# Decoder trunk on one core: regrouping the last third of the down projections, and a new place for twelve conditioning columns

## The chip, the core and the metric

The kernel is one program on one NeuronCore of a Trainium2 chip. The metric is the device time of one execution, in microseconds, as the median of several runs. Besides that time there is one profiled execution, whose trace gives each instruction's start, length and engine: PE (TensorE matmuls), PEld (its weight loads), DVE (VectorE), ACT (ScalarE), POOL (GpSimd) and SP (SyncE, which here only issues DMAs).

## What is computed

The reference is a decoder trunk of two layers on a sequence of 512 tokens with 1024 channels. Each layer has three sub-layers, and each of them is normalised with a shift, a scale and a gate that come from a conditioning vector `c`:

```python
cond = jax.nn.silu(c)
for l in range(DEPTH):                                   # 2
    mod = cond @ ada_w[l] + ada_b[l]                     # 9 * 1024 values
    sh1, sc1, g1, sh2, sc2, g2, sh3, sc3, g3 = jnp.split(mod, N_MOD, axis=-1)
    h = modulate(x, norm_ffn1[l], sh1, sc1)
    x = x + 0.5 * (1.0 + g1)[:, None] * swiglu(h, ffn1_w1[l], ffn1_w3[l], ffn1_w2[l])
    h = modulate(x, norm_mix[l], sh2, sc2)
    y = token_mix(h, ...)          # gated delta rule and latent attention, two branches, gated, then w_out
    x = x + (1.0 + g2)[:, None] * y
    h = modulate(x, norm_ffn2[l], sh3, sc3)
    x = x + 0.5 * (1.0 + g3)[:, None] * swiglu(h, ffn2_w1[l], ffn2_w3[l], ffn2_w2[l])
```

`swiglu(h, w1, w3, w2)` is `(silu(h @ w1) * (h @ w3)) @ w2` with an inner width of 2816, that is 22 tiles of 128. `modulate` is an RMS norm over the channels, times a gain and `1 + scale`, plus a shift. Everything is in float32.

## The kernel before, in words

**Layout and precision.** Activations are held channel-major: a tile is 128 channels by 512 tokens. Every large product is done three times in the matmul's reduced fp32 type. Weights and activations are split into a high part (a cast on ACT) and a low part (a subtraction on DVE), and `mm3` adds high times high, high times low and low times high into one PSUM bank. A block of weights, called a slab, is 128 partitions by up to 1024 columns, that is up to eight blocks of 128x128, one for each `k` of a reduction. `slab` (L114) loads it with a DMA on SP's queue into a buffer `raw` (or `L`), and makes `whi` on ACT (L121) and `wlo` on DVE (L122), in two pieces of up to 512 columns each. There are two `raw`, three `whi`, three `wlo` and five `L` buffers.

**PSUM.** The eight banks are shared out by name: three `acc`, two `sm`, two `sc`, one `po` (`BUFS`).

**One FFN** (`ffn`). The 22 inner tiles are made in thirds of 8, 8 and 6. The tiles of a third are made by `pairs` (two inner tiles together, in seven products of half size, casts at L582 and L583 from slabs of 1024 columns, outputs to `x`, `y` and `z` in `acc`, `sm` and `sc`). The last step of a pair ends with a Silu of `x` on ACT (L633), a product on DVE (L638), and the split of the second inner tile (ACT L135, DVE L136). After each third, `down(i)` multiplies these inner tiles (`xs`, in buffers `O`) with the slabs of `w2`, one slab for each of the eight output tiles `m`, and adds the gated result to `x` (`residual`, L407, on DVE). This is done by `close`.

**`close`** (L410). For the first two thirds all eight `m` are done one after the other over all 512 tokens. For the last third four `m` are done so; the slabs of the other four are put into `spare` places in the buffers `A` (loaded through `L`), and these four are then done in two halves of 256 tokens, so that the norm of the first half can start while the second half is multiplied. The first half's banks are all `acc`, the second half's all `sc`. `finish` squares the new `x` on ACT (L320, L323) and adds the squares on DVE (L324). `NORM_AT` says after which `k` the norm's small matmuls are put in. `ahead` loads the next stage's first slabs. The same `close` with spare slabs in `O` does the output projection `w_out` at the end of the mixing.

**The conditioning columns.** A column of 128 values of `mod` is one `ada_block` (L264): a DMA of 512 KB into an `L` buffer and one DVE instruction (L269) that multiplies it with the conditioning vector `condb` (buffer `kph`) and sums. Its place in DVE's order is pinned by `order`. Per layer, 48 such columns (j from 2 to 7, eight each) wait in a queue before the first FFN; with layer 0's position tables that is 49 entries. `tick(n)` pops n of them at set places: two for each tile or pair of the upper projections, two or one for each output tile of the first two thirds, one for each of the last third's four. What is left is drained before the mixing.

**The order of the work.** The kernel is written with a scheduling layer. It takes instructions in the order in which they are written as priority, but an engine whose next instruction isn't ready by its estimate gets a later one that is, and a buffer goes to the instruction that asks for it when it comes free. The order so found is fixed in the program: on the chip each engine runs its list strictly in order, and each DMA queue too. `keep_in_program_order` (`order`, and `pin` for matmuls) puts an instruction behind the one that was written just before it for the same engine.

**The end of the mixing** (`mix`, L1267). After the attention, for each of eight tiles `m`: a slab of `w_branch_b`, a load of a stored gate, 24 matmuls, a product with the gate on DVE (L1416), an addition on POOL (L1417), and a split (L135, L136) into the buffers `A`. Then `x` comes back from memory and `close` does `w_out`. After the mixing `condb` is loaded again, since `kph` was lent to the attention.

Of the kernel before, what the change touches and what calls it, by code (L numbers as in the profile page):

```python
# [8 lines left out]
F32 = mybir.dt.float32  # L9
# [6 lines left out]
P = 128  # L16
SEQ = 512
D = 1024
# [16 lines left out]
HALVES = ((0, 256), (256, 512))  # L35
# [15 lines left out]

BEGIN_PE = (1, 2)

WQ, WK, WV, WZ, WLAT, WMISC, WGA, WGB = 0, 8, 16, 24, 32, 37, 38, 46
N_WIN = 54

# [17 lines left out]
class Trunk:  # L74
    def __init__(self, ctx, tc, aps):
        self.tc = tc
        self.nc = tc.nc
        self.ap = aps
        self.sb = ctx.enter_context(tc.tile_pool(name="sb", bufs=1))
        self.ps = ctx.enter_context(tc.tile_pool(name="ps", bufs=1, space=bass.MemoryType.PSUM))  # L80
        self.count = 0
        self.pin = False
        self.units, self.body, self.ahead = [], None, None
        self.queue = []
        self.waiting = []
        self.quarters = {}
# [24 lines left out]
        return self.ps.tile(list(shape), F32, tag=tag, name=f"{tag}_{self.count}", bufs=BUFS[tag])  # L111


    def slab(self, src, n, place=None, home="raw"):  # L114
        nc = self.nc
        raw = self.t(home, [P, 1024])
        hi, lo = place or (self.t("whi", [P, 1024], F32R), self.t("wlo", [P, 1024], F32R))
        nc.sync.dma_start(raw[:, :n], src)
        for a in range(0, n, 512):
            s = slice(a, min(a + 512, n))  # L120
            nc.scalar.copy(hi[:, s], raw[:, s])  # L121
            nc.vector.tensor_sub(lo[:, s], raw[:, s], hi[:, s].bitcast(F32))  # L122
        return hi, lo

    def mm3(self, out, w, x, start, stop):
# [137 lines left out]

    def ada_block(self, l, j, i, mod):  # L264

        raw = self.t("L", [P, D])
        self.nc.sync.dma_start(raw, self.ap["ada_w"][l, j, i])
        o = j * KT + i
        self.order(self.nc.vector.scalar_tensor_tensor(raw, raw, 1.0, self.condb, ALU.mult, ALU.mult,  # L269
                                                       accum_out=mod[:, o:o + 1]))  # L270
# [136 lines left out]
        self.nc.vector.scalar_tensor_tensor(self.x[:, m, a:b], ps[:, a:b], gate[:, m:m + 1], self.x[:, m, a:b],  # L407
                                            ALU.mult, ALU.add)

    def close(self, get, acts, gate, finish, spare=(), ahead=None, ticks=(1, 1)):  # L410

        late = KT - len(spare)
        for m in range(late):
            s = get(m)
            ps = self.p("acc")
            self.proj(ps, s, acts)
            self.residual(m, ps, gate, FULL[0])
            if finish is not None:
                finish(m, FULL[0])
            self.tick(ticks[m % 2])  # L420
# [1 line left out]
        if ahead is not None:  # L422
            ahead()
        norms = []
        for (a, b), tag in zip(HALVES if ws else (), ("acc", "sc")):
            for m, s in zip(range(late, KT), ws):
                ps = self.p(tag)
                n = len(acts)

                cut = NORM_AT.get(m - late, n) if norms else n  # L430
                self.proj(ps, s, acts, (a, b), range(cut))
                if cut < n:
                    next(norms[0], None)
                    self.proj(ps, s, acts, (a, b), range(cut, n))
                self.residual(m, ps, gate, (a, b))
                norm = finish(m, (a, b))
                if norm is not None:
                    norms.append(norm)
# [50 lines left out]
    def ffn(self, l, w, gate, finish, early, ahead=None):  # L489
# [199 lines left out]
        def down(i):  # L689
            k0, k1 = THIRDS[i]  # L690
            xs = [g[k] for k in range(k0, k1)]
            get = lambda m, place=None: self.slab(w2[l, m, :, k0:k1, :].rearrange("p k c -> p (k c)"), (k1 - k0) * P,
                                                  place, "L" if place else "raw")
            spare = []
            if i == 2:
                for _ in range(2):
                    sp = self.t("A", [P, 4, 1024], F32R)
                    spare += [(sp[:, 0], sp[:, 1]), (sp[:, 2], sp[:, 3])]
            self.close(get, xs, gate, finish if i == 2 else None, spare, ahead if i == 2 else None,
                       (1, 1) if i == 2 else (2, 1))  # L700

        begun = len(early) > 3
        plain = 6 if begun else 4
# [562 lines left out]

    def mix(self, l, vec, gate, finish, ws, ahead):  # L1267
        nc = self.nc
        xs = self.ap["spill"]
        for k in range(KT):  # L1270
            nc.sync.dma_start(xs[:, k, :], self.x[:, k, :])
# [132 lines left out]
        self.fill_all()  # L1404
        for cur in wait:
            next(cur, None)
        yh = self.t("A", [P, KT, SEQ], F32R)
        yl = self.t("A", [P, KT, SEQ], F32R)
        for m in range(KT):
            w = self.slab(self.ap["w_branch_b"][l, m].rearrange("p k c -> p (k c)"), 1024)  # L1410
            gate_b = self.t("c3", [P, SEQ])
# [4 lines left out]
            nc.vector.scalar_tensor_tensor(y, gate_b, 1.0, ps, ALU.add, ALU.mult)  # L1416
            nc.gpsimd.tensor_add(y, y, t1[0][:, m, :])  # L1417
            self.split(yh[:, m, :], yl[:, m, :], y)
        ys = [(yh[:, k, :], yl[:, k, :]) for k in range(KT)]
        self.x = self.t("M", [P, KT, SEQ])  # L1420
        for k in range(KT):
# [97 lines left out]
    def run(self, out):  # L1519
# [12 lines left out]
        for l in range(DEPTH):  # L1532
# [11 lines left out]

            for j in range(2, 8):
                self.queue += self.ada_chunk(l, j, vec, mod)
            if l == 0:
                self.queue.insert(10, self.rope_tables)
            g1 = {}
            self.ffn(l, "ffn1", _Lazy(lambda: self.set_gate(0, mod)), done(1, vec, mod),  # L1550
                     early if l == 0 else nxt["w"], then(self.mix_early, l))
            self.drain()
            self.mix(l, vec, self.set_gate(1, mod), done(2, vec, mod), nxt["w"], then(self.ffn_early, l, "ffn2"))
            self.condb = self.t("kph", [P, D])
            nc.sync.dma_start(self.condb, self.ap["spill_c"])
            self.queue += self.ada_chunk(l, 8, vec, mod)
            if l + 1 < DEPTH:
                nvec, nmod = self.layer_vectors(l + 1)
# [111 lines left out]
```

## Time and profile before

| | |
|---|---|
| median of 3 runs | 2739.33 us (2736.4 to 2739.42) |
| profiled execution | 2742.08 us |
| its span, first to last instruction | 2740.3 us |
| its mean granted TensorE clock | 0.998 |
| instructions | 44511 |
| DVE L269, conditioning columns | 142 instructions, 169.9 us |
| ACT L121, slabs' casts in pieces | 554 instructions, 320.0 us |
| DVE L122, slabs' low parts in pieces | 554 instructions, 387.9 us |
| DMA over the span | 394.66 MB, mean 144 GB/s |

Four stretches are the last thirds: they start at about 344 us (layer 0, first FFN), 1345 us (layer 0, second), 1703 us (layer 1, first) and 2703 us (layer 1, second). The branch-B loop of layer 0 lies between about 941 and 982 us. A busy time is the sum of an engine's instructions; matmuls overlap one another, so PE's pace is read from start to start. A row of a timeline gives the start, the length, the engine, the line, the operation, what it writes and reads (out<-in), and in brackets how long the engine had been idle before and what ended that.

### The profile page before, as it was taken

Reading aid. Unit: us, or ns where it says so; the run is one execution under the profiler, and the core shown is the slowest. Engines: PE = TensorE matmul, PEld = TensorE weight load, DVE = VectorE, ACT = ScalarE, POOL = GpSimd, SP = SyncE. Lnnn points to the kernel's source line nnn. Section 1 sums busy time; section 2 is a strip of 40 time slices with the busy share of each in tenths; the row PEclk is TensorE's granted clock in tenths of the full one; section 3 lists DMA queues with packets and bytes.
Section 4 is the critical chain, followed back from the end, with each engine's and each line's share of the span. In section 5 each row is a group of like instructions: output and inputs, shape, how many; then the busy total and the mean of one; then the engine's idle time right before and its main releaser. Section 6 shows DMA issues by size and latency. Waiting matters only on the chain.

```text
span 2740.3 us, 44511 instructions
## 1 busy us (share of the span) xinstructions
PE 2695.0 (98%) x17168; PEld 2396.7 (87%) x17168; DVE 2006.5 (73%) x4025; ACT 1285.4 (47%) x2519; POOL 266.9 (10%) x390
## 2 busy tenths in 40 slices
PE   7999999999999999999999999999999999999999
PEld 6989988788888788998889999887888888898988
DVE  6877877777668767875678878786767686685755
ACT  5534345444446535443445344545434564453533
POOL 0000015000001011000010000150000111110000
PEclk9999999999999999999999999999999999999999
DMA  8678733222222453885528777322222224456642
GB/s 308 184 224 236 239 125 111 90 69 81 67 79 71 131 177 114 247 232 146 158 67 229 244 231 235 97 100 89 74 81 71 76 78 125 156 153 185 161 131 86
DMA packets 118869, 394.66 MB, mean 144 GB/s; under 512 B 13440, under 2 KB 16128, under 8 KB 118656
## 3 DMA queue, kind: packets, MB, share of 16 engines
q1 hardware_dynamic: 106128, 350.38, 38.7%
q0 software_dynamic: 10080, 36.70, 7.5%
q10 hardware_dynamic: 2448, 4.72, 0.4%
q8 instruction: 135, 2.21, 0.3%
q14 instruction: 78, 0.64, 0.1%
HBM read 376.55 MB, written 15.20 MB: 143 GB/s over the span
## 4 chain that ended last, share of the span: by engine, by line
PE 82%; DVE 9%; issue 3%; ACT 3%; POOL 2%; DMA 1%; SPq 0%; ACTq 0%; POOLq 0%; DVEq 0%
PE acc L94 57%; PE sc L94 16%; PE sm L94 5%; PE sm L99 2%; DVE wlo L122 2%; PE po L94 1%; DVE cv L729 1%; DVE L L861 1%; DVE L L863 1%; POOL g L821 0%; ACT whi L121 0%; POOL g L823 0%; POOL O L842 0%; DMA raw<-in_w_in 0%; ACT hhi L389 0%
## 5 line engine op out<-in xcount | busy, mean ns | idle before, releaser
L121 ACT CAST whi<-raw 128x512 fp32r<-128x512 f32 (+2 forms) x554 | 320.0, 607 | 429.2 <-PE acc L94 241.1
L94 PE MATMUL acc<-hhi,whi 128*128 128x512 f32 (+1 forms) x1368 | 506.3, 371 | 11.1 <-DVE cv L729 5.8
L94 PE MATMUL acc<-hlo,whi 128*128 128x512 f32 (+1 forms) x1368 | 487.6, 357 | 1.2 <-POOL hlo L392 0.3
L94 PE MATMUL acc<-hhi,wlo 128*128 128x512 f32 (+1 forms) x1368 | 486.7, 356 | 0.0
L122 DVE TENSOR_TENSOR wlo<-raw,whi 128x512 fp32r<-128x512 f32 (+2 forms) x554 | 387.9, 719 | 107.8 <-ACT whi L121 101.0
L94 PE MATMUL acc<-O,whi 128*128 128x512 f32 x1472 | 456.3, 391 | 2.7 <-ACT O L135 2.2
L94 PE MATMUL acc<-A,whi 128*128 128x256 f32 (+1 forms) x1808 | 346.6, 291 | 0.7 <-ACT g L653 0.5
L94 PEld LDWEIGHTS acc<-O,whi 128*128 128x128 f32 x1472 | 275.9, 188 | 60.4 <-ACT O L135 2.6
L94 PEld LDWEIGHTS acc<-hhi,whi 128*128 128x128 f32 x1368 | 259.5, 190 | 42.4 <-issue 8.3
L94 PEld LDWEIGHTS acc<-hhi,wlo 128*128 128x128 f32 x1368 | 259.4, 190 | 37.3 <-DVE wlo L1491 0.2
L94 PEld LDWEIGHTS acc<-A,whi 128*128 128x128 f32 x1808 | 286.0, 192 | 6.2 <-ACT g L653 0.9
L94 PEld LDWEIGHTS acc<-hlo,whi 128*128 128x128 f32 x1368 | 260.3, 190 | 31.7 <-POOL hlo L392 3.0
L94 PE MATMUL acc<-O,wlo 128*128 128x512 f32 x736 | 287.3, 390 | 0.0
L94 PE MATMUL acc<-A,wlo 128*128 128x256 f32 (+1 forms) x904 | 262.6, 290 | 0.0
L582 ACT CAST whi<-L 128x1024 fp32r<-128x1024 f32 x140 | 147.0, 1050 | 205.0 <-issue 77.0
L583 DVE TENSOR_TENSOR wlo<-L,whi 128x1024 fp32r<-128x1024 f32 x140 | 171.3, 1224 | 35.3 <-ACT whi L582 34.6
L94 PEld LDWEIGHTS acc<-A,wlo 128*128 128x128 f32 x904 | 173.3, 192 | 2.5
L269 DVE SCALAR_TENSOR_TENSOR L<-L,kph 128x1024 f32<-128x1024 f32 x142 | 169.9, 1220 | 5.0 <-DMA L<-in_ada_w 5.0
L583 DVE TENSOR_TENSOR wlo<-raw,whi 128x1024 fp32r<-128x1024 f32 x105 | 128.6, 1224 | 59.1 <-ACT whi L582 58.1
L557 POOL DMA_DIRECT2D L<-in_ffn_w x70 | 61.1, 873 | 1086.0 <-DMA L<-in_ffn_w 459.7
L582 ACT CAST whi<-raw 128x1024 fp32r<-128x1024 f32 x105 | 110.2, 1049 | 118.9 <-PE acc L94 49.3
L94 PEld LDWEIGHTS acc<-O,wlo 128*128 128x128 f32 x736 | 138.5, 188 | 28.9
(432 smaller groups left out, 5339.5 us busy)
## 6 DMA issues: line engine op xcount, KB each, us to landing
raw<-in_ffn_w SPq DMA_DIRECT2D x166, 512.0 KB, 4.3
L<-in_ada_w SPq DMA_DIRECT2D x142, 512.0 KB, 5.0
raw<-in_w_in SPq DMA_DIRECT2D x108, 512.0 KB, 3.4
L<-in_ffn_w SPq DMA_DIRECT2D x105, 512.0 KB, 4.5
L<-in_ffn_w POOLq DMA_DIRECT2D x70, 512.0 KB, 8.4
raw<-in_w_branch_a SPq DMA_DIRECT2D x16, 512.0 KB, 3.4
raw<-in_w_branch_b SPq DMA_DIRECT2D x16, 512.0 KB, 3.7
raw<-in_w_out SPq DMA_DIRECT2D x16, 512.0 KB, 3.5
```

The source lines that it names most:

```text
L94: i = self.nc.tensor.matmul(*a, **k)
L99: i = self.nc.tensor.transpose(*a, **k)
L121: nc.scalar.copy(hi[:, s], raw[:, s])
L122: nc.vector.tensor_sub(lo[:, s], raw[:, s], hi[:, s].bitcast(F32))
L269: self.order(self.nc.vector.scalar_tensor_tensor(raw, raw, 1.0, self.condb, ALU.mult, ALU.mult, accum_out=mod[:, o:o + 1]))
L557: nc.gpsimd.dma_start(t, w13[l, m2, half2].rearrange("p w k c -> p (w k c)"), accum_op=ALU.add)
L582: nc.scalar.copy(hi, t)
L583: nc.vector.tensor_sub(lo, t, hi[:].bitcast(F32))
L729: nc.vector.scalar_tensor_tensor(acc[:, s:], ps[:, :SEQ - s], w[j], acc[:, s:], ALU.mult, ALU.add)
L861: nc.vector.tensor_mul(tv, f[:, j + 1:, j:j + 1].to_broadcast([P, n, w]), x[:, j:j + 1, :w].to_broadcast([P, n, w]))
L863: nc.vector.tensor_sub(x[:, j + 1:, :w], x[:, j + 1:, :w], tv)
```

## The change

- `slab` makes one cast and one subtraction of the whole slab where `wide` is set. It is set except from the start of the mixing to the end of its attention.
- In the last third of every down projection the casts and subtractions of slabs 0, 1 and 2 are pinned behind what was written before them on ACT and DVE (`hold`).
- There, `close` takes the first two slabs and two `acc` banks at once, multiplies k 0 to 3 for both output tiles, and then k 4 and 5 for both (`early` = 4).
- The half-width tiles use the banks acc, acc, acc, sc for the first half and sc, acc, sc, sc for the second, in both uses of `close`.
- The last third pops no conditioning columns. The last twelve columns of each layer (the second half of j = 6 and all of j = 7) are taken out of the queue of the first FFN and popped, two and one by turns, in the branch-B loop at the end of the mixing. There they are loaded into `O` buffers instead of `L`, and `condb` is loaded again before that loop and no longer after the mixing.

```diff
+PUT_OFF = 12
...
+    def slab(self, src, n, place=None, home="raw", hold=False):
...
-        for a in range(0, n, 512):
-            s = slice(a, min(a + 512, n))
-            nc.scalar.copy(hi[:, s], raw[:, s])
-            nc.vector.tensor_sub(lo[:, s], raw[:, s], hi[:, s].bitcast(F32))
+        w = 1024 if self.wide else 512
+        for a in range(0, n, w):
+            s = slice(a, min(a + w, n))
+            both = [nc.scalar.copy(hi[:, s], raw[:, s]),
+                    nc.vector.tensor_sub(lo[:, s], raw[:, s], hi[:, s].bitcast(F32))]
+            for i in both if hold else ():
+                self.order(i)
...
-        raw = self.t("L", [P, D])
+        raw = self.t(self.ada_home, [P, D])
...
+        lead = 2 if early else 0
+        ws = [get(m) for m in range(lead)]
+        pss = [self.p("acc") for _ in ws]
+        for ks in (range(early), range(early, len(acts))) if lead else ():
+            for s, ps in zip(ws, pss):
+                self.proj(ps, s, acts, ks=ks)
         for m in range(late):
-            s = get(m)
-            ps = self.p("acc")
-            self.proj(ps, s, acts)
+            if m >= lead:
+                s = get(m)
+                ps = self.p("acc")
+                self.proj(ps, s, acts)
+            else:
+                ps = pss[m]
             self.residual(m, ps, gate, FULL[0])
...
-        for (a, b), tag in zip(HALVES if ws else (), ("acc", "sc")):
+        tags = iter(("acc", "acc", "acc", "sc", "sc", "acc", "sc", "sc"))
+        for a, b in HALVES if spare else ():
             for m, s in zip(range(late, KT), ws):
-                ps = self.p(tag)
+                ps = self.p(next(tags))
...
-                                                  place, "L" if place else "raw")
+                                                  place, "L" if place else "raw", i == 2 and m < 3)
...
-                       (1, 1) if i == 2 else (2, 1))
+                       (0, 0) if i == 2 else (2, 1), 4 if i == 2 else None)
...
+        self.wide = True
+        self.condb = self.t("kph", [P, D])
+        nc.sync.dma_start(self.condb, self.ap["spill_c"])
...
+        self.ada_home = "O"
         for m in range(KT):
             w = self.slab(self.ap["w_branch_b"][l, m].rearrange("p k c -> p (k c)"), 1024)
...
+            self.tick(2 - m % 2)
+        self.drain()
+        self.ada_home = "L"
...
+            self.queue, put_off = self.queue[:-PUT_OFF], self.queue[-PUT_OFF:]
...
             self.drain()
+            self.queue += put_off
             self.mix(l, vec, self.set_gate(1, mod), done(2, vec, mod), nxt["w"], then(self.ffn_early, l, "ffn2"))
-            self.condb = self.t("kph", [P, D])
-            nc.sync.dma_start(self.condb, self.ap["spill_c"])
```

More of the change, by code (lines that the diff above doesn't have):

```diff
@@ L111, in p @@
         return self.ps.tile(list(shape), F32, tag=tag, name=f"{tag}_{self.count}", bufs=BUFS[tag])
-    def slab(self, src, n, place=None, home="raw"):
+    def slab(self, src, n, place=None, home="raw", hold=False):
         nc = self.nc
@@ L408, in residual, with close @@
                                             ALU.mult, ALU.add)
-    def close(self, get, acts, gate, finish, spare=(), ahead=None, ticks=(1, 1)):
+    def close(self, get, acts, gate, finish, spare=(), ahead=None, ticks=(1, 1), early=None):
         late = KT - len(spare)
-        for m in range(late):
-            s = get(m)
-            ps = self.p("acc")
-            self.proj(ps, s, acts)
+        lead = 2 if early else 0
[4 more added lines that the diff above has]
+                self.proj(ps, s, acts, ks=ks)
+        for m in range(late):
+            if m >= lead:
[4 more added lines that the diff above has]
+                ps = pss[m]
             self.residual(m, ps, gate, FULL[0])
@@ L1268, in mix @@
         nc = self.nc
+        self.wide = False
         xs = self.ap["spill"]
@@ L1406, in mix @@
             next(cur, None)
+        self.wide = True
+        self.condb = self.t("kph", [P, D])
+        nc.sync.dma_start(self.condb, self.ap["spill_c"])
         yh = self.t("A", [P, KT, SEQ], F32R)
         yl = self.t("A", [P, KT, SEQ], F32R)
+        self.ada_home = "O"
         for m in range(KT):
@@ L1418, in mix @@
             self.split(yh[:, m, :], yl[:, m, :], y)
+            self.tick(2 - m % 2)
+        self.drain()
+        self.ada_home = "L"
         ys = [(yh[:, k, :], yl[:, k, :]) for k in range(KT)]
```

## The prediction

> **What bounds the kernel now.** I read the page first, then the view of waits on PE, then PE's timeline around each wait, and last the other engines at those places.
>
> ```profile
> span 2740.3 us, 44511 instructions
> ...
> PE 2695.0 (98%) x17168; PEld 2396.7 (87%) x17168; DVE 2006.5 (73%) x4025; ACT 1285.4 (47%) x2519; POOL 266.9 (10%) x390
> ```
>
> PE is the bound. An edit can only pay where PE stands still or runs slowly, and two of the longest waits lie in last thirds of down projections:
>
> ```profile
> PE acc L94 <- ACT O L135: 2.2, 1, 2.2
> PE acc L94 <- DVE M L407: 2.2, 1, 2.2
> ```
>
> The second is in layer 0's first FFN, where the half-width tiles run (PE's timeline, start and length in us):
>
> ```profile
> 360.28 6.64 PE L94 MATMUL acc<-O,A 128*128 128x256 f32 x54
> 366.76 0.88 PE L94 MATMUL sc<-O,A 128*128 128x256 f32 x6
> 369.80 3.77 PE L94 MATMUL acc<-O,A 128*128 128x256 f32 x18 [2.16 <-DVE M L407]
> 373.41 0.76 PE L94 MATMUL sc<-O,A 128*128 128x256 f32 x5
> ```
>
> At pace, 54 matmuls take 366.76-360.28 = 6.48, or 0.120 each. After the six on "sc" the fourth "acc" tile should start at 367.48; it starts 2.32 later. Its 18 matmuls then take 3.61 instead of 2.16, another 1.45. The first wait is where layer 0's second FFN enters its last third:
>
> ```profile
> 1344.86 0.63 PE L94 MATMUL acc<-O,whi 128*128 128x512 f32 x2
> ...
> 1348.06 0.39 PE L94 MATMUL acc<-O,wlo 128*128 128x512 f32 x1
> 1350.66 0.49 PE L94 MATMUL acc<-O,whi 128*128 128x512 f32 x1 [2.21 <-ACT O L135]
> ...
> 1356.18 0.40 PE L94 MATMUL acc<-O,wlo 128*128 128x512 f32 x1
> ```
>
> Fourteen matmuls from 1344.86 to 1348.06 give 0.229 each. The next comes 2.37 late, and the 14 from 1350.66 to 1356.18 take 5.52 instead of 3.21: 2.31 more. Both slow stretches have a lower granted clock (PEclk, the third column from the end):
>
> ```profile
> 365.00:375.00 10.00, 7.84 (x54) 7.67 (x54) 7.46 (x16) 2.08 (x5) 0.00 (x0) 0.83 0.32 113
> 1346.00:1358.00 12.00, 9.45 (x33) 7.09 (x32) 5.10 (x10) 4.75 (x11) 0.54 (x1) 0.86 0.93 263
> ```
>
> So a gap of 2.3 costs 3.8 to 4.7. [...] The same entry of layer 1's first FFN loses 0.86-2x0.229 = 0.40; the last FFN's shows no wait in the list:
>
> ```profile
> 1706.81 1.03 PE L94 MATMUL acc<-O,whi 128*128 128x512 f32 x2
> 1707.67 0.40 PE L94 MATMUL acc<-O,wlo 128*128 128x512 f32 x1
> ```
>
> To be won at most: 3.77 + 4.68 + 0.40 = 8.85.
>
> **The change, part by part.** The wait at 369.80 is a bank's: the fourth "acc" tile needs the first one's residual, and DVE runs that late.
>
> ```profile
> 364.67 0.69 DVE L324 TENSOR_TENSOR g<-g,g 128x512 f32<-128x512 f32 x1 [0.85 <-ACT g L323]
> 365.28 1.22 DVE L269 SCALAR_TENSOR_TENSOR L<-L,kph 128x1024 f32<-128x1024 f32 x1
> ...
> 366.43 1.02 DVE L122 TENSOR_TENSOR A<-L,A 128x512 fp32r<-128x512 f32 x2
> 367.37 1.89 DVE L122 TENSOR_TENSOR wlo<-raw,whi 128x512 fp32r<-128x512 f32 x3
> 369.17 1.26 DVE L407 SCALAR_TENSOR_TENSOR M<-acc,gate,M 128x256 f32<-128x256 f32 x3
> ```
>
> The rotation gives the fourth tile an "sc" bank, which is free, and the next tile that reuses an "acc" bank comes two tiles (36x0.120 = 4.3) later. The conditioning column (L269, 1.22) is gone from this place too: layer 0's queue shrinks from 49 entries to 37 and layer 1's from 48 to 36, and by the code's ticks 40 and 42 have been popped when the second third ends, so no column is left for the last one. Next late would be the residuals themselves, with 4.3 of room. Gain 3.77, nothing left over.
>
> The wait at 1350.66 is an order on ACT:
>
> ```profile
> 1345.06 0.38 ACT L633 ACTIVATE cv<-acc 128x256 f32<-128x256 f32 x1 [0.60 <-PE acc L94]
> 1349.17 0.92 ACT L121 CAST whi<-raw 128x512 fp32r<-128x512 f32 x2 [3.72 <-DMA raw<-in_ffn_w]
> 1350.00 0.61 ACT L135 CAST O<-g 128x512 fp32r<-128x512 f32 x1
> ```
>
> The third slab's cast stands ahead of the last activation's cast (L135) and waits 3.72 for its DMA; PE waits for the activation. "hold" pins the casts of slabs 0 to 2 behind everything traced before them on ACT and DVE, so this cannot recur: gain 4.68, and the 0.40 of layer 1 likewise.
>
> But the pin also holds slabs 0 and 1, which are now cast before the pairs end. This is the added wait. Slab 0's cast must follow the last activation's. The row at 1345.06 starts that chain; it is 0.38 long, so the product follows about 0.42 later, and the cast 0.45 after the product's start, by:
>
> ```profile
> 345.32 0.42 DVE L638 SCALAR_TENSOR_TENSOR g<-acc,cv 128x256 f32<-128x256 f32 x1
> ...
> 345.77 0.62 ACT L135 CAST O<-g 128x512 fp32r<-128x512 f32 x1 [0.52 <-DVE g L638]
> ```
>
> then 0.61, then slab 0 in one piece of 768 columns, between 0.61 and 1.05 on ACT (0.84) and between 0.63 and 1.22 on DVE (0.95), by:
>
> ```profile
> L582 ACT CAST whi<-raw 128x1024 fp32r<-128x1024 f32 x105 | 110.2, 1049 | 118.9 <-PE acc L94 49.3 <-issue 42.4 <-DVE raw L592 15.0
> L583 DVE TENSOR_TENSOR wlo<-raw,whi 128x1024 fp32r<-128x1024 f32 x105 | 128.6, 1224 | 59.1 <-ACT whi L582 58.1
> ```
>
> That is, 1345.06+0.42+0.45+0.61+0.84+0.95 = 1348.3 for a low part that PE now takes at 1345.3: 3.0 per entry, four entries. Uncovered, with 1.45 to 2.31 of slow clock, 4.5 to 5.3 each, 18 to 21 in all. What can lie over it is work from further on: tiles 4 and 5 of the halves need only slabs in "A", and these are cast ahead where the "L" buffers are free (first row), late where conditioning columns hold them (second row):
>
> ```profile
> 1334.90 1.76 ACT L121 CAST A<-L 128x512 fp32r<-128x512 f32 x4
> ...
> 354.12 0.62 ACT L121 CAST A<-L 128x512 fp32r<-128x512 f32 x1 [0.84 <-DMA L<-in_ffn_w]
> ```
>
> With the columns moved, all four entries should look like the first row. Two half tiles without their last k are 2x15x0.120 = 3.6, more than 3.0; two "acc" banks are free at that time. And the scheduler does draw PE work forward over a known wait: it put the branch projection (acc<-O) between attention's last steps.
>
> ```profile
> 936.57 0.71 PE L94 MATMUL acc<-O,whi 128*128 128x512 f32 x2
> ...
> 938.57 0.71 PE L94 MATMUL acc<-O,whi 128*128 128x512 f32 x2
> ```
>
> So I take 0.2 per entry (between 0 and 5.3), 0.8 in all, nearest to the covered end. If the split into k 0-3 and 4-5 then shares no wait, because the pinned slabs come after both late activations, it costs nothing either.
>
> "wide" makes one cast of two: an edit at nothing, hidden behind PE; without that cover a slab's first matmul waits up to 1.05-0.61 + 1.22-0.63 = 1.0 longer.
>
> The twelve columns go to the branch-B loop: per layer 12 DMAs of 512 KB on SP's queue, ahead of later slabs, and 12 L269. Their bytes, 6.3 MB over eight tiles of 24x0.229 = 5.5, add 143 GB/s to a loop like the first row here; the second shows that PE stayed busy beside 297 GB/s. Both rows count us, busy times, clock, DMA share, GB/s.
>
> ```profile
> 960.00:980.00 20.00, 20.00 (x90) 16.55 (x89) 13.84 (x15) 6.74 (x12) 6.53 (x4) 1.00 0.31 101
> ...
> 350.00:360.00 10.00, 10.00 (x46) 8.29 (x45) 9.33 (x17) 5.83 (x11) 0.00 (x0) 1.00 0.95 297
> ```
>
> On DVE a tile now takes 0.60 + 2.39 + 0.60 = 3.6 of 5.5, and 1.5 columns at 1.15 (365.28 to 366.43) make it 5.3:
>
> ```profile
> 955.46 0.69 DVE L1416 SCALAR_TENSOR_TENSOR g<-c,acc 128x512 f32<-128x512 f32 x1 [1.62 <-PE acc L94]
> 956.06 2.39 DVE L122 TENSOR_TENSOR wlo<-raw,whi 128x512 fp32r<-128x512 f32 x2
> ...
> 956.28 1.62 POOL L1417 TENSOR_TENSOR g<-g,M 128x512 f32<-128x512 f32 x1 [3.82 <-DVE g L1416]
> ```
>
> The two casts take 2.39 instead of 1.2 beside POOL's add. [...] Behind the last pinned column stands the next L1416, for which the output projection's eighth k waits:
>
> ```profile
> 985.79 0.69 DVE L136 TENSOR_TENSOR A<-g,A 128x512 fp32r<-128x512 f32 x1
> ...
> 982.46 0.61 PE L94 MATMUL acc<-A,whi 128*128 128x512 f32 x2
> ```
>
> PE takes that low part 22 matmuls after 982.46, at 987.5; it is there at 986.5, so 1.0 of room, and DVE idles 1.62 before each L1416. Two columns (2.3) can use that up and leave 0 to 1.3, with 1.45 of slow clock at worst: 0 to 2.8 per layer. I take 0.5, as the idle 1.62 covers most of it; 1.0 for two layers. A gain is excluded, since PE has no wait here now. The conditioning vector's reload moves with the columns, ahead of the loop's first slabs on SP's queue:
>
> ```profile
> kph<-spill_c SPq DMA_DIRECT2D x2, 512.0 KB, 3.2
> ```
>
> It lies under attention's last steps; without that cover it costs its 3.2 once per layer.
>
> Sum: -8.85 + 0.8 + 1.0 = -7.05. The profiled execution took 2742.08 (its span and 1.8 around it), 2.75 above the median of 2739.33. Against its own time the sum gives 2735.0; against the median, 2732.3.
>
> **Rivals.** (1) The pins cost PE their wait at all four entries. For it: a cast that today precedes the pairs' end may no longer do so. Against: the work drawn forward above. It decides when less than about 1 us is covered: -8.85 + 18 to 21 + 1.0, about 2751, slower. (2) One half tile covers and the other has no bank: 3.0-1.8 = 1.2 open, and 0.7 of slow clock; four times 1.9 = 7.6, which gives 2739.1, no change. For it: only three "acc" banks. (3) The mixing's end becomes DVE's: if POOL's add blocks a column as it blocks the cast (1.1 more), a tile takes 6.4 on DVE against 5.5; 16x0.9 = 14.4, so -8.85+0.8+14.4, 2745.7. Against: POOL adds once per tile. (4) The shared wait does not exist, as said above; then pin and rotation alone give the forecast, and it has no time of its own.
>
> **Numbers.** Forecast 0.52, (1) 0.20, (2) 0.20, (3) 0.08. What a measurement can tell from no change is about 0.2%, 5.5 us. The forecast's own range is 2728 to 2737: from 2730.5 with no cost at all, less the 3 us by which the runs shown differ, to costs of 6.5 of the 9.6 that entries at up to 1.0 and loops at up to 2.8 would add; some 0.08 of its 0.52 lies within 0.2%. Faster 0.45, same 0.26, slower 0.29. The range, 2728 to 2750, takes in (2), (3) and the near half of (1).
>
> **What would show it.** Right: no wait of PE on L407 or L135, clock 1.00 in all four last thirds, matmuls acc<-O,A ahead of the first acc<-O,whi at the entries, PE without a break in the branch-B loop. Wrong: PE waiting on the slab helper's whi or wlo casts at the entries (rival 1, or 2 where the wait is under 2 us), or L1416 starting more than 1 us after its tile (3). If the waits are gone and the time has not moved, the sum is wrong and not a term.

## The result, and the profile after

The changed kernel takes 2769.95 us (median of 4 runs, 2766.46 to 2773.34) beside 2738.4 for the kernel before on the same chip: a ratio of 1.0118, 95% interval 1.0102 to 1.0134. It is slower by 1.2%. The prediction had 2732.3, and a range that ended at 2750.

The page of the profiled execution, which is the fastest of its four:

```profile
span 2764.7 us, 44191 instructions
...
PE 2700.9 (98%) x17168; PEld 2397.6 (87%) x17168; DVE 1980.0 (72%) x3862; ACT 1266.6 (46%) x2356; POOL 272.9 (10%) x390
```

DVE and ACT do less than before (1980.0 for 2006.5, 1266.6 for 1285.4), and the span is 24.4 longer. PE and POOL run the same number of instructions as before (17168 and 390) and show 6 more of busy time each. So no engine got more work; the order got worse. The waits of PE by what it waited for (us in total, times, longest):

```profile
PE acc L98 <- ACT whi L127: 9.8, 4, 2.4
PE acc L98 <- ACT A L143: 9.6, 2, 5.1
PE sc L98 <- DVE wlo L128: 1.6, 3, 0.5
PE acc L98 <- DVE wlo L128: 1.2, 2, 0.9
```

The two waits that the prediction wanted gone (on the activation's cast and on the residual) are gone. Four new ones of 2.4 on slab casts are the four entries of the last thirds, and two of about 5 are the two ends of the mixing. They appear in the same order in PE's timeline. First the entry of layer 0's second FFN, where PE stood from 1354.8 to 1357.39:

```profile
1354.67 0.28 PE L98 MATMUL acc<-A,wlo 128*128 128x256 f32 x1
1357.39 1.47 PE L98 MATMUL acc<-O,whi 128*128 128x512 f32 x4 [2.44 <-ACT whi L127]
1358.70 0.41 PE L98 MATMUL acc<-O,wlo 128*128 128x512 f32 x1
```

ACT at that place (the first row is 10 earlier), and then DVE's row for the low part of slab 0:

```profile
1344.82 1.57 ACT L127 CAST A<-L 128x768 fp32r<-128x768 f32 x2
...
1354.99 0.38 ACT L652 ACTIVATE cv<-acc 128x256 f32<-128x256 f32 x1 [0.62 <-PE acc L98]
1355.27 0.82 ACT L127 CAST A<-L 128x768 fp32r<-128x768 f32 x1
1355.99 0.62 ACT L143 CAST O<-g 128x512 fp32r<-128x512 f32 x1
1356.51 1.57 ACT L127 CAST whi<-raw 128x768 fp32r<-128x768 f32 x2
```

```profile
1357.60 1.82 DVE L128 TENSOR_TENSOR wlo<-raw,whi 128x768 fp32r<-128x768 f32 x2
```

This is the chain that the prediction worked out: activation 1354.99, its cast 1355.99, slab 0's cast 1356.51. The slabs of half tiles 4 and 5 are cast in time, as assumed (the two "A<-L" from 1344.82; the one at 1355.27 is the third of the four slabs). But no matmul on them stands in PE's gap. The half tiles come after slabs 0 and 1 are done:

```profile
1365.99 2.55 PE L98 MATMUL sc<-O,A 128*128 128x256 f32 x20
```

Then the end of the mixing in layer 0. DVE's timeline of two turns of the loop (L1440 makes y, L128 is the next slab's low part, L144 y's low part, L277 the columns):

```profile
963.43 1.22 DVE L277 SCALAR_TENSOR_TENSOR O<-O,kph 128x1024 f32<-128x1024 f32 x1
...
964.77 1.22 DVE L277 SCALAR_TENSOR_TENSOR O<-O,kph 128x1024 f32<-128x1024 f32 x1
...
965.92 0.68 DVE L1440 SCALAR_TENSOR_TENSOR g<-c,acc 128x512 f32<-128x512 f32 x1
966.52 1.22 DVE L128 TENSOR_TENSOR wlo<-raw,whi 128x1024 fp32r<-128x1024 f32 x1
969.57 0.69 DVE L144 TENSOR_TENSOR A<-g,A 128x512 fp32r<-128x512 f32 x1 [1.84 <-ACT A L143]
970.18 1.22 DVE L277 SCALAR_TENSOR_TENSOR O<-O,kph 128x1024 f32<-128x1024 f32 x1
...
971.32 0.68 DVE L1440 SCALAR_TENSOR_TENSOR g<-c,acc 128x512 f32<-128x512 f32 x1
```

POOL's add and ACT's cast of the same turn, and what PE saw after the last turn:

```profile
966.68 2.21 POOL L1441 TENSOR_TENSOR g<-g,M 128x512 f32<-128x512 f32 x1 [4.54 <-DVE g L1440]
```

```profile
968.92 0.62 ACT L143 CAST A<-g 128x512 fp32r<-128x512 f32 x1 [5.18 <-POOL g L1441]
```

```profile
993.49 1.52 PE L98 MATMUL acc<-A,whi 128*128 128x512 f32 x2 [5.06 <-ACT A L143]
```

DVE is idle for 1.84 in each turn between the first and the last (the bracket at L144), so it isn't short of time. The turn is a ring: y (965.92), POOL's add (966.68), ACT's cast (968.92), y's low part (969.57), one or two columns pinned behind it (970.18), and only then the next y (971.32). With one column that is 5.41, with two 6.56 to 6.75. PE needs 24x0.229 = 5.5 per tile. The first turn takes 8.38, as POOL's first add starts only at 948.58, behind a DMA issue (L576) in POOL's own list; the seven turns from 945.38 to 989.85 take 44.5, where at PE's pace (5.44 from y to y with the columns back, below) they take 38.1. The y's fall 6.4 behind, until PE has nothing left to do but wait for the last. Its first two matmuls after that take 1.52 (993.49) where two took 0.61 before (986.66), with the granted clock at 0.50 until 998.21.

**Where the 24 went.** PE executes the same 17168 matmuls in both kernels. The table compares the start of matmuls of the same number with the trace of before, and gives by how many us each stretch became longer (+) or shorter. A third is counted with the norm behind it, and the last column holds what lies between the stretches too. The experiments' kernels, told below, stand in it as well.

| kernel (profiled execution) | layer 0 FFN1 third | layer 0 mixing's end | layer 0 FFN2 third | layer 1 FFN1 third | layer 1 mixing's end | layer 1 FFN2 third | all |
|---|---|---|---|---|---|---|---|
| changed | -0.6 | +8.0 | -0.6 | +4.3 | +7.9 | +3.0 | +24.0 |
| no pins | -3.8 | +7.5 | -3.8 | -0.4 | +7.5 | -0.2 | +9.6 |
| columns back | +6.7 | +0.7 | +0.9 | +6.9 | +0.2 | +4.6 | +25.1 |
| columns before split | -0.6 | +0.5 | +0.8 | +3.8 | +0.7 | +4.6 | +13.5 |
| two-piece casts | -0.5 | +2.1 | -0.3 | +4.4 | +2.8 | +4.2 | +13.2 |
| no cut | +3.7 | +8.4 | +1.4 | +5.6 | +8.0 | +4.7 | +32.8 |
| no rotation | -0.4 | +8.6 | -2.6 | +4.1 | +6.9 | +0.2 | +20.7 |
| sc first | -3.3 | +8.3 | -3.4 | +0.1 | +7.9 | +0.2 | +11.8 |
| pins alone | +9.0 | 0.0 | +1.3 | +11.7 | +0.1 | +0.6 | +19.7 |
| rotation alone | -3.5 | 0.0 | -2.8 | 0.0 | +0.1 | 0.0 | -7.6 |
| columns alone | -3.6 | +1.9 | -0.4 | -0.2 | +3.9 | 0.0 | -1.5 |
| three repairs | -3.8 | +2.0 | -4.8 | -0.4 | +0.4 | -0.2 | -8.0 |
| eight columns | -3.8 | 0.0 | -4.8 | -0.4 | +0.1 | -0.2 | -9.5 |
| eight columns, no cut | -3.5 | 0.0 | -2.2 | -0.2 | 0.0 | 0.0 | -5.0 |
| wide casts alone | -2.2 | +0.3 | -2.0 | +0.2 | +0.2 | +0.3 | +0.7 |

The median moved by 31.5, the profile by 24.4. The profiled execution of before is 3.7 above the 2738.4, and that of after 3.5 below its own median; that is the 7.2 between the two. The profiled execution of after has a mean granted clock of 0.997, its three others 0.995. So the table compares a long execution of before with a short one of after, and gains look larger in it than in the medians.

### The profile page after: what moved, and what is told of

It is laid out like the page before. It is cut to its first block, busy times and chain, and to the rows that moved or that the text cites. A ratio compares the mean times of both kernels' runs of the same rounds, so it can differ in the third digit from the quotient of the medians.

```text
span 2764.7 us, 44191 instructions
## 1 busy us (share of the span) xinstructions
PE 2700.9 (98%) x17168; PEld 2397.6 (87%) x17168; DVE 1980.0 (72%) x3862; ACT 1266.6 (46%) x2356; POOL 272.9 (10%) x390
## 3 DMA queue, kind: packets, MB, share of 16 engines
q8 instruction: 135, 2.21, 0.3%
## 5 line engine op out<-in xcount | busy, mean ns | idle before, releaser
L98 PE MATMUL acc<-hhi,whi 128*128 128x512 f32 (+1 forms) x1368 | 505.8, 371 | 10.8 <-DVE cv L748 5.5
L127 ACT CAST whi<-raw 128x512 fp32r<-128x512 f32 (+4 forms) x415 | 304.4, 747 | 401.2 <-PE acc L98 198.9
L128 DVE TENSOR_TENSOR wlo<-raw,whi 128x512 fp32r<-128x512 f32 (+4 forms) x415 | 356.1, 864 | 130.7 <-ACT whi L127 122.1
L602 DVE TENSOR_TENSOR wlo<-L,whi 128x1024 fp32r<-128x1024 f32 x140 | 171.2, 1223 | 37.1 <-ACT whi L601 35.7
L415 DVE SCALAR_TENSOR_TENSOR M<-acc,gate,M 128x512 f32<-128x512 f32 (+1 forms) x112 | 77.3, 691 | 135.4 <-PE acc L98 133.2
L576 POOL DMA_DIRECT2D L<-in_ffn_w x70 | 60.9, 871 | 1058.2 <-DMA L<-in_ffn_w 414.9
```

The lines of the kernel that those rows point to most:

```text
L98: i = self.nc.tensor.matmul(*a, **k)
L127: both = [nc.scalar.copy(hi[:, s], raw[:, s]), nc.vector.tensor_sub(lo[:, s], raw[:, s], hi[:, s].bitcast(F32))]
L576: nc.gpsimd.dma_start(t, w13[l, m2, half2].rearrange("p w k c -> p (w k c)"), accum_op=ALU.add)
L602: nc.vector.tensor_sub(lo, t, hi[:].bitcast(F32))
```

## The experiments

The theory: (a) the pins cost about 3 at each entry because nothing is drawn forward over them, for want of a free bank; (b) the columns behind the low part close a ring in the mixing's loop; (c) the wide casts lengthen that ring and a few first low parts. Each run's time is a median beside the kernel before on the same chip (2737.9 to 2739.9).

### No pins

```diff
-place, "L" if place else "raw", i == 2 and m < 3)
+place, "L" if place else "raw", False)
```

> The casts of slabs 0 to 2 of the last third keep no place; all else as in the changed kernel. Theory A (the pins put slab 0's cast behind the last product, and PE has nothing to draw forward): the four gaps of 2.6 us with 0.4 to 0.5 of slow clock go, 12 us in all: 2769.9-12 = 2758; if the old wait of layer 0's second FFN on the activation's cast comes back (4.7), 2763. Rival (the gaps come from the first two tiles being traced together, or from the slabs' transfers): the gaps stay and the time stays within 3 us of 2770.

Measured: 2752.12, ratio 1.0056 (1.0044 to 1.0069): theory A, and 6 faster than its 2758. The waits on slab casts are gone at all four entries; in the table 3.2, 3.2, 4.7 and 3.2 come back, 14.3 in all. PE starts slab 0 right behind the last products (343.08), because the cast stands ahead of the last activation again (ACT's timeline of this kernel):

```profile
343.20 0.83 ACT L127 CAST whi<-raw 128x768 fp32r<-128x768 f32 x1
343.94 0.38 ACT L652 ACTIVATE cv<-acc 128x256 f32<-128x256 f32 x1
```

The old wait of 4.7 in layer 0's second FFN has not come back, so something other than the pin keeps it away (see the version without the cut).

### Columns back in the first FFN

```diff
-(0, 0) if i == 2 else (2, 1), 4 if i == 2 else None)
+(1, 1) if i == 2 else (2, 1), 4 if i == 2 else None)
...
-            self.tick(2 - m % 2)
```

with `put_off` and the early reload of `condb` taken out as well.

> The twelve columns of each layer go back into the first FFN's queue (ticks 1,1 in its last third) and the conditioning vector is read back after the mixing, as before. Theory A (the columns lengthen the loop of the mixing's end by 8 us per layer): 2769.9-16 = 2754, and up to 2758 if the wait in layer 0's half tiles (3.8) returns; y steps 5.4 us apart again. Rival (the loop is slow through the wide casts beside POOL's add): no more than 3 us come back, 2767 or later, with the steps still 5.9 us apart on average.

Measured: 2766.15, ratio 1.0105 (1.0089 to 1.0120). Only 3.8 came back, and the rival's number (2767) is nearer than the theory's 2754; yet the rival is wrong too. The loop is cured: its y's start 5.44 apart, and the table has 0.7 and 0.2 in place of 8. What it gave went elsewhere, most of it to the entries: the thirds of the two first FFNs stand at 6.7 and 6.9, where the changed kernel has -0.6 and 4.3. DVE there:

```profile
347.11 1.22 DVE L277 SCALAR_TENSOR_TENSOR L<-L,kph 128x1024 f32<-128x1024 f32 x1
...
348.25 1.22 DVE L277 SCALAR_TENSOR_TENSOR L<-L,kph 128x1024 f32<-128x1024 f32 x1
...
349.39 1.82 DVE L128 TENSOR_TENSOR wlo<-raw,whi 128x768 fp32r<-128x768 f32 x2
```

Two columns pinned ahead of slab 0's pinned low part make it 2.3 later still, and PE waits a second time at that entry. With pins, the columns had to leave the last third.

### Columns before the split

```diff
-            self.split(yh[:, m, :], yl[:, m, :], y)
             self.tick(2 - m % 2)
+            self.split(yh[:, m, :], yl[:, m, :], y)
```

> In the loop of the mixing's end the columns are traced ahead of the split of y, so they stand on VectorE between the gated sum's first step and the low part, where VectorE idles 1.84 us per tile. Theory A1 (it is the order: the columns stand behind the low part and ahead of the next y): the loop is PE's again with 5.4 us per tile, 2769.9-15 = 2755. Theory A2 (VectorE's two-input step and POOL's add shut each other out, so the idle 1.84 can't be used): POOL's add starts or ends 1.1 to 2.3 later, the chain per tile stays at about 5.9, and the time is 2767 to 2772.

Measured: 2756.11, ratio 1.0065 (1.0052 to 1.0077): A1. The same instructions with one line moved, and the loop's 15.9 fall to 1.2. DVE's turn, where the columns now fill the time in which POOL and ACT work on y:

```profile
962.88 0.68 DVE L1440 SCALAR_TENSOR_TENSOR g<-c,acc 128x512 f32<-128x512 f32 x1
963.47 1.22 DVE L277 SCALAR_TENSOR_TENSOR O<-O,kph 128x1024 f32<-128x1024 f32 x1
...
964.62 2.31 DVE L128 TENSOR_TENSOR wlo<-raw,whi 128x1024 fp32r<-128x1024 f32 x1
966.85 0.68 DVE L144 TENSOR_TENSOR A<-g,A 128x512 fp32r<-128x512 f32 x1
967.61 0.69 DVE L1440 SCALAR_TENSOR_TENSOR g<-c,acc 128x512 f32<-128x512 f32 x1
```

L144 finds its input ready and the next y follows it directly. The lengthening that A2 counts on is there (L128 takes 2.31 instead of 1.22), but it fits into the turn: L1440 starts 4.57 to 5.79 apart after the first turn.

### Two-piece casts

```diff
-        w = 1024 if self.wide else 512
+        w = 512
```

> Each slab is cast in two pieces of 512 everywhere, as before; all else as in the changed kernel. Theory A (the one wide cast makes the first low part late in some places, 0.4 to 1.05 each, and lengthens slab 0's pinned chain by 0.4 to 0.6 at each entry): 2769.9-5 = 2765. Rival 1 (the wide casts also hold up POOL's add in the mixing's loop, 2.15 instead of 1.62): up to 8 more come back, 2757. Rival 2 (they cost nothing, being hidden behind PE): within 2 us of 2770.

Measured: 2753.63, ratio 1.0062 (1.0049 to 1.0074): rival 1. In the loop 11 of the 15.9 come back, outside it little, and the entries keep their cost. POOL's add in this kernel:

```profile
963.82 1.68 POOL L1441 TENSOR_TENSOR g<-g,M 128x512 f32<-128x512 f32 x1 [4.55 <-DVE g L1440]
968.76 1.61 POOL L1441 TENSOR_TENSOR g<-g,M 128x512 f32<-128x512 f32 x1 [3.27 <-DVE g L1440]
```

It ends 0.5 earlier, the ring takes 4.88 or 6.02 (once 6.22), and 5.49 on average after the first turn is about PE's own pace.

### No cut after the fourth k

```diff
-(0, 0) if i == 2 else (2, 1), 4 if i == 2 else None)
+(0, 0) if i == 2 else (2, 1), None)
```

> Tiles 0 and 1 of the last third are no longer taken together with their sum cut after the fourth k; the pins and all else stay. Theory A (behind the pin both late activations are cast before slab 0 is, so the cut shares no wait, and the half tiles find no bank either way): within 3 us of the changed kernel's 2770, the four gaps of 2.6 still there. Rival (taking two banks at once is what keeps the half tiles from being drawn forward): the four gaps go, 2758.

Measured: 2775.49, ratio 1.0129 (1.0116 to 1.0143). Neither. The gaps at the entries stay, so taking two banks at once isn't what keeps the half tiles back; but the time is 5.5 longer. The waits of PE in this kernel have a row for the scale of the norm at the FFN's end:

```profile
PE po L98 <- DVE nv L347: 4.4, 8, 1.1
```

In the changed kernel the same row has 0.9 in all. So part of the loss lies at the thirds' ends, where half tiles should lie over the norm of the first half; that the cut changes which half tiles are left by then is only argued.

### No rotation

```diff
-("acc", "acc", "acc", "sc", "sc", "acc", "sc", "sc")
+("acc", "acc", "acc", "acc", "sc", "sc", "sc", "sc")
```

> The half tiles keep acc four times and sc four times, as before. Theory A (the conditioning column is gone from this place, so the residual that the fourth half tile waits for is early): no wait on the residual, 2770 within 3 us. Rival (the rotation is what removes the wait of 3.8 in layer 0, as the prediction had it): the wait is back there and perhaps in the other three last thirds, 2774 to 2785.

Measured: 2760.88, ratio 1.0075 (1.0061 to 1.0089), faster than the change by 9 (by 3.3 between the two profiles), which neither side expected. PE at the entry of layer 0's first FFN:

```profile
345.91 0.28 PE L98 MATMUL acc<-A,wlo 128*128 128x256 f32 x1
346.03 2.85 PE L98 MATMUL sc<-O,A 128*128 128x256 f32 x21
348.73 0.66 PE L98 MATMUL acc<-O,whi 128*128 128x512 f32 x2
```

Here is the cover that the prediction counted on: 21 half-tile matmuls, no gap. By their tag they are tiles of the second half, the first two (4 and 5), whose slabs are cast first. The new rotation gives the first "sc" bank to tile 7 of the first half, whose slab is the last of the four to be cast, and tiles 4 to 6 of the first half get "acc" banks, which come round behind the whole tiles. So the rotation itself took the cover away. But the same work then lacks at the third's end, where it used to lie over the norm:

```profile
382.30 0.71 PE L98 MATMUL po<-const,nv 128*128 128x128 f32 x4 [1.39 <-DVE nv L347]
...
384.13 0.62 PE L98 MATMUL acc<-hhi,whi 128*128 128x256 f32 x3 [1.11 <-ACT hhi L397]
```

There is one reserve of work and two places that want it. The residual's wait (2.2 in the prediction) isn't there either, without the rotation.

### sc first

```diff
-tags = iter(("acc", "acc", "acc", "sc", "sc", "acc", "sc", "sc"))
+tags = iter(("sc", "sc", "acc", "acc", "acc", "sc", "sc", "acc") if early else ("acc", "acc", "acc", "sc", "sc", "acc", "sc", "sc"))
```

> The half tiles of the last thirds with a cut take sc, sc, acc, acc and then acc, sc, sc, acc; the pins stay. Theory A (the half tiles could not be drawn forward because an acc bank that they would take is, in order of rotation, one of a whole tile that is not done; the sc banks are free): some 20 matmuls of the half tiles stand between the last product and the first one of slab 0, the four gaps of 2.6 go, 2770-12 = 2758, or -10 if the sc banks are short later. Rival (the half tiles' own slabs are not ready then): the gaps stay, 2770.

Measured: 2753.27, ratio 1.0048 (1.0036 to 1.0061): theory A, 16.7 faster than the change with every pin in place. PE's entry in layer 0's first FFN:

```profile
344.19 2.85 PE L98 MATMUL sc<-O,A 128*128 128x256 f32 x21
346.89 0.66 PE L98 MATMUL acc<-O,whi 128*128 128x512 f32 x2
```

It draws the first half's tiles forward and leaves the second half's for the norm, so all four thirds come out within 0.5 of those without pins (-3.3, -3.4, +0.1, +0.2). As nothing but the tags moved, the slabs of the half tiles were not what kept them back.

### Each part alone on the kernel before

The pins alone:

```diff
+            for i in both if hold else ():
+                self.order(i)
```

> The kernel before with the casts of slabs 0 to 2 of the last thirds held in their place, and nothing else. Theory A (the sc bank is free for the second half's first tile, as the banks are the old ones, so the second FFNs' entries, which have no columns, are covered by sc matmuls and only the old wait of 4.7 goes; in the first FFNs columns hold the buffers of the half tiles' slabs, so nothing is ready to be drawn forward and each entry costs 3 and up to 7): 2738.3-4.7+6 to 14 = 2740 to 2748. Rival (a pin costs its 3.0 at all four entries whatever the banks): waits on slab casts at all four, 2738.3-4.7+12 = 2746.

Measured: 2762.67, ratio 1.0086 (1.0072 to 1.0100): worse than either bound. The half right is that the second FFNs' entries are covered by "sc" matmuls. The price went to the end of the thirds. PE at the end of layer 0's second FFN in this kernel, and the clock there (the 0.65):

```profile
1389.02 0.61 PE L94 MATMUL sm<-ones,g 128*128 128x1 f32 x4 [0.91 <-DVE g L326]
1391.28 1.01 PE L94 MATMUL sm<-ones,g 128*128 128x1 f32 x4 [1.66 <-DVE g L326]
1393.60 1.22 PE L94 MATMUL po<-const,nv 128*128 128x128 f32 x4 [1.31 <-DVE nv L341]
1395.93 0.58 PE L94 MATMUL acc<-hhi,whi 128*128 128x256 f32 x1 [1.11 <-ACT hhi L391]
```

```profile
1392.00:1405.00 13.00, 10.58 (x63) 10.20 (x63) 9.47 (x36) 8.10 (x20) 2.20 (x3) 0.65 0.00 1
```

And the first FFNs, with columns in the way, lose 9.0 and 11.7.

The rotation alone (the tags, as in the diff of the change):

> The kernel before with the half tiles' new banks (acc, acc, acc, sc, then sc, acc, sc, sc) and nothing else. Theory A (the rotation takes the wait of 3.8 in layer 0's first FFN away by itself, and as nothing is pinned here no cover is needed at the entries): 2738.3-3.8 = 2734.5. Rival (the column that stands ahead of the residual sets that wait, whatever the banks): the wait stays, 2738; above 2740 would mean that the lost sc bank costs here too.

Measured: 2734.63, ratio 0.9981 (0.9973 to 0.9990): theory A. Where nothing is pinned no cover is needed, and the bank alone takes the wait away (-3.5 in the table); the other wait, in the second FFN, shrank to 1.0 as well.

The columns alone (behind the split, two-piece casts):

> The kernel before with the twelve columns of each layer at the mixing's end, behind the split, and nothing else (two-piece casts, no pins, old banks, no cut). Theory A (the chain POOL, ScalarE, low part, columns is 5.5 to 6.1 per tile with two-piece casts; what the run with two-piece casts left of the loop's 8 is 2 to 3.3 per layer; the residual's wait goes with the column): 2738.3+5.3-3.8 = 2740, or 2735 if the wait on the activation's cast goes too. Rival (the columns cost nothing without the wide casts): 2734.5.

Measured: 2741.96, ratio 1.0006 (0.9997 to 1.0015): theory A. The loop costs 1.9 and 3.9, and 3.6 comes back in layer 0's first FFN, this time because the column is gone. Either edit removes that wait, so their gains don't add.

The wide casts alone:

```diff
+        w = 1024 if self.wide else 512
+        for a in range(0, n, w):
```

> The kernel before with a slab cast in one piece (two pieces still in the mixing up to its end), and nothing else. Theory A (the wide casts cost by themselves only where a first low part comes late, 4 to 5 us over the kernel, and the rest of the 16 that two-piece casts brought back stems from the loop with the columns, where POOL's add starts 0.6 late): 2739+4.5 = 2743. Rival (they cost wherever they stand): 2750 to 2755.

Measured: 2745.61, ratio 1.0030 (1.0019 to 1.0041), between theory A's 2743 and the rival's 2750, nearer the former: by themselves they cost some 8 of the 16. The trace shows 2.9 of these. At the start of three FFNs PE waits 0.30 for a slab's cast and then for its low part, and loses 0.95 each time, as it does in the changed kernel:

```profile
1049.52 0.50 PE L95 MATMUL sc<-hhi,wlo 128*128 128x512 f32 x1 [0.53 <-DVE wlo L124]
```

Where the rest lies is open: the profiled execution, at 2742.8, is low among its runs, that of before is high among its own, and PE ends only 0.7 later than before's.

### Versions without the costs

Three repairs: no pins, columns before the split, two-piece casts.

> No pins, the columns ahead of the split, and two-piece casts, with the rotation, the cut after k 3 and the columns' new place kept. Theory A (three costs with separate places: 14 at the entries, 14 in the loop, 5 through the wide casts outside the loop): the sum, 2766.5-14-14-5 = 2733 in the profiled execution, 2732 to 2740. Rival (two of the costs hide behind each other, as the loop's share came back in the run with two-piece casts too): 2740 to 2748.

Measured: 2734.83, ratio 0.9986 (0.9977 to 0.9995). The sum held to 2 us, with the wide casts counted only outside the loop. Inside the loop their cost and the columns' overlap: one repair at a time gains 14.4, 10.5 and 10.8 in the table, 35.7 in all, and the three together 32.0.

Eight columns, one per turn, in that version:

```diff
-PUT_OFF = 12
+PUT_OFF = 8
...
-            self.tick(2 - m % 2)
+            self.tick(1)
```

> As the version with no pins, columns ahead of the split and two-piece casts, but eight columns per layer instead of twelve go to the mixing's end, one per tile. Theory A (a tile with two columns is what still lengthens the loop there, by 1.65 and 1.06 per layer; four more columns end in the first FFN's second third): 2734.8-2.7 = 2732. Rival (the four columns reach the last third again and bring back a wait of up to 3.8): 2735 to 2739.

Measured: 2732.25, ratio 0.9970 (0.9958 to 0.9982), the fastest here, faster than both kernels. The loop costs nothing now (0.0 and 0.1).

The same without the cut:

> As the version with eight columns, but tiles 0 and 1 of the last third are not taken together and not cut after the fourth k. Theory A (without pins slabs 0 and 1 are cast before the last activations, so the cut could share a wait here, but no wait of PE is left at the entries to be shared): 2732 within 2 us. Rival (the cut is what keeps the last activation's wait of 4.7 in layer 0's second FFN away once the pins are gone): the wait is back, 2735 to 2737.

Measured: 2736.71, ratio 0.9995 (0.9986 to 1.0003): the rival. The wait is back in layer 0's second FFN, 1.63 for the activation's cast, which again stands on ACT behind a slab that waits for its transfer:

```profile
1344.99 0.92 ACT L127 CAST whi<-raw 128x512 fp32r<-128x512 f32 x2 [3.14 <-DMA raw<-in_ffn_w]
1345.82 0.61 ACT L143 CAST O<-g 128x512 fp32r<-128x512 f32 x1
```

With the cut, PE has 27 matmuls (k 0 to 3 of both tiles and k 4 of the first, 6.2) before it needs that cast, instead of a single tile's 15 (3.4); the wait goes, though the order on ACT is the same. In the version with the cut the cast also ends 1.0 sooner after PE's first matmul on the slab, for a reason that was not looked into; by those times a single tile's 15 would still have waited 0.7.

## Why the prediction was wrong

**The gains.** 8.85 was named, and the thirds without pins show 3.8+3.8+0.4 = 8.0, those of the three repairs 3.8+4.8+0.4+0.2 = 9.2. In the profile the place and the size were right; by the medians the best version gains 7.7 in all (2732.25 beside 2739.92). Who earns them was half right: the residual's wait goes with the rotation alone (-3.5) and with the columns' move alone (-3.6), and the wait on the activation's cast goes with the cut, without a pin. "The shared wait does not exist" holds only behind the pins; without them it is worth 2.6 in that third and 4.5 in the profile and in the medians (these from two chips).

**The first step that failed: "So I take 0.2 per entry".** The chain to 1348.3 was right, and so, nearly, was its length of 3.0: beside the version without pins the entries cost 3.2, 3.2, 4.7 and 3.2, that is 14.3 for the 0.8 taken. PE waited on the slabs' casts, as the prediction's own sign of being wrong has it. What failed is "two acc banks are free at that time". A bank is handed out in the order in which the tiles are traced, so the half tiles' "acc" banks belong to whole tiles not yet done. The free banks are "sc", and the rotation, which the prediction booked as pure gain, moved the first of these to a tile whose slab is late (its cast starts at 1357.98 in layer 0's second FFN, behind the gap). That the "acc" banks are held is read from the code; that the tags decide is shown by two runs: with the old tags the cover is there and the gap gone, and with "sc" first the gap is gone at all four. Why the second "sc" bank, which falls to tile 4 of the second half, wasn't used at the entry either is not settled.

Rival 1 had the right event at too high a price for this execution: 14.3 where it had 18 to 21. It charged 1.45 to 2.31 of slow clock at each gap, and the granted clock fell to 0.50 behind one of the four only, for 3.41 (the entry that cost 4.7; see the last section). Behind the others PE's first four steps take 1.31-4x0.229 = 0.4 more than at pace (1357.39 to 1358.70), at a granted clock of 1.00. The other executions, with their clock of 0.995, may have paid more of it; they have no trace. Rival 2 named the cause, no bank, but for one of the two half tiles; here neither was drawn forward.

**The second: "I take 0.5, as the idle 1.62 covers most of it".** It cost 8.0 and 7.9 per layer, against a bound of 2.8. The step added up DVE's busy time per tile (5.3 of 5.5) and set the columns against DVE's idle time. But the columns are pinned behind L144, and L144 waits for POOL and ACT. An idle engine whose next instruction in order waits isn't free. The sum that decides is the ring's, from start to start: y to add 0.76, add to cast 2.24, cast to low part 0.65, low part to column 0.61, column to the next y 1.14. That is 5.4 for one column and, with 1.15 more, 6.6 for two, against PE's 5.44. The six turns after the first lose 3.5 by it, and the first, where the late add holds up the whole ring, 2.9. The same columns ahead of the split cost 1.2 in both layers together. Rival 3 named the engine and 14.4 for the sum, near the 15.9, but by busy time; DVE idles 1.84 per turn, so its mechanism was not the one, and the nearness of the number is luck.

**The third: '"wide" makes one cast of two: an edit at nothing'.** In the ring it costs 11 of the 15.9: POOL's add takes 2.21 beside one piece and 1.68 beside two. By itself it measures about 8, of which the trace shows 2.9: the 0.95 at the start of three FFNs, where the "1.0 longer" that the prediction named for a slab without cover was paid.

**The sum.** -9.2 of gains (the thirds of the three repairs), +14.3 at the entries, +15.9 in the loop, +2.9 for the wide casts at the start of three FFNs and +0.1 elsewhere give the 24.0 of the profile. The missing terms came from one habit: a cost was set to nothing since something idle lay beside it, without asking whether that idle thing could be used in that order.

## What to carry to other kernels

Before booking a pinned instruction as hidden, follow the ring that it stands in (each hand-over from engine to engine until the same instruction comes again) and compare that with the bound engine's pace; idle time of an engine counts only if its next instruction in order is ready (here DVE's 1.84 per turn did only for columns ahead of the split). Before counting on work that is drawn forward, name its bank and its operand and who holds them, and ask which later place loses that work. Edits that take away the same wait don't add, and a pin that cures a wait of 4.7 once at a price of 3 four times is a loss; here it was enough to give PE more to do before it asks.

## What the runs showed of the hardware

- Beside each other, POOL's add and DVE's subtraction of a slab took longer in the branch-B loop, in one kernel the one, in one the other. In the kernel before, the two pieces of layer 0's loop take 1.29 in the first turn (945.18), ahead of the add, and 2.39 in the next (950.62), beside an add of 1.68 (950.78). In the changed kernel the one wide piece keeps its 1.22 (966.52) and the add beside it takes 2.21 (966.68); in the first turn, where the add starts after the subtraction has ended at 947.45, it takes 1.59 (948.58). What decides which of the two takes longer is not shown.
- A gap alone doesn't tell the clock. In the traces of the two kernels the granted clock is 1.00 but for three stretches at 0.50 in each and the changed kernel's last 1.8 us. The 0.83 and 0.86 beside the waits of 2.2 in the kernel before are one stretch of 3.41 within 10 (from 369.53) and one of 3.41 within 12 (from 1352.57). The four entries of the changed kernel have the same wait of 2.44; behind the third (1711.37 to 1713.81) the clock stood at 0.50 for 3.41, from 1715.01 on, behind the three others at 1.00. Around the first and behind the third:

```profile
344.00:352.00 8.00, 5.56 (x27) 4.19 (x27) 5.28 (x7) 4.29 (x7) 0.00 (x0) 1.00 0.27 85
```

```profile
1715.01:1718.42 3.41, 3.41 (x10) 2.73 (x9) 1.70 (x2) 0.22 (x1) 0.00 (x0) 0.50 0.67 214
```

With the wait of 5.06 at layer 0's mixing's end it was 0.50 for 6.83, from 991.38 on (the 0.61 below), and with the four waits of 0.91 to 1.66 of the pins alone its mean from 1392 to 1405 was 0.65 (above). What decides between the equal waits is not settled here.

```profile
990.00:996.00 6.00, 2.51 (x5) 1.78 (x6) 3.83 (x7) 1.57 (x2) 2.93 (x2) 0.61 0.40 81
```

- The mean granted clock of an execution is 0.995 to 0.997 in the runs of the changed kernel, 0.994 to 0.995 with pins alone, and 0.999 to 1.000 in those of the version with eight columns (medians 2769.95, 2762.67 and 2732.25).
